# Output projection with earlier weight splits and delayed squares, and first GLA states copied on another engine

## The chip, the cores and the metric

The kernel runs on one core of one Trainium2 chip. The metric is the device time of one execution in microseconds (us); the median of several runs counts. Work is done by five engines, each with an instruction queue of its own that it works off in order: TensorE (PE in the profile; its weight loads are PEld), VectorE (DVE), ScalarE (ACT), GpSimd (POOL) and SyncE (SP, which here issues most DMAs). They wait for each other by semaphores.

## The reference

One decoder layer with two parallel branches, a retention and a gated linear attention (GLA), merged by sigmoid gates, then an output projection, the residual and a final RMS norm. D_MODEL is 1024, the sequence 512 with 16 meta tokens ahead of it, all in float32:

```python
u = rms_norm(h, norm_gain)
proj = u @ w_in            # rq, rk, rv, rg, gq, gk, gv, gg, glr, m_ret, m_gla
o_ret = retention_chunked(rope(rq), rope(rk) * scale, rv)
o_ret = head_group_norm(o_ret, ret_norm_gain) * silu(rg)
o_gla = gla_chunked(gq * scale, gk, gv, log_a)
o_gla = head_rms_norm(o_gla, gla_norm_gain) * silu(gg)
merged = sigmoid(m_ret) * (o_ret @ w_branch_ret) + sigmoid(m_gla) * (o_gla @ w_branch_gla)
h = h + merged @ w_out
out = rms_norm(h, final_norm_gain)[:, N_META:]
```

In the GLA scan each head carries a state (128 x 256) from block to block: `state = state * exp(a_n) + k_n^T v_n`. The kernel computes its first value from the meta tokens.

## The kernel before

**Float32 in three products.** Each operand is split in a high half (a cast to fp32r, on ScalarE) and a low half (operand minus high half, on VectorE): `split`, L164. A product is then three matmuls: high by high, high by low, low by high. For a weight tile of 128 x 1024 a split is one ScalarE CAST and one VectorE TENSOR_TENSOR.

**Seven products for eight.** `quad` (L267) computes a 2 x 2 block product with seven block products in place of eight. It loads the weight blocks w11, x3, w21, x1 and w22 (raw tiles; x3 and x1 get a second block added by an accumulating DMA from GpSimd), forms sums of them on VectorE (L388: w11 += x3; L395: w21 += w11) and runs the products in the order 1, 2, 6, 7, 5, 4, 3. They accumulate in three PSUM banks: 1, 6, 5 and 3 in `b` (the later ones on top of the earlier), 2 in `a`, 7 and 4 in `c`. After some of them bank contents are copied out on ScalarE (`copy`, L345 and L348) or handed to the caller's evacuation (`put`, which calls `evac`). `prepare(i, w)` takes a pair of weight buffers and issues the split of product i's weight, and notes it in `low`; without an earlier `prepare`, `product` issues it itself. There are three such pairs (`whi`, `wlo`, `bufs=3`), handed out in turn, so the split of one product has to wait until the product three before it is done. The flag `ahead` (set for retention heads 0 and 3, in their gate projection rg) issues the splits of products 2 and 4 sooner, `sooner` that of 6, `early` another order.

**Order of the work.** `weave(dense, chain)` runs a dense generator (a quad) and after each of its yields one step of a chain (other work), so the code's order is an interleaving of the two. `pend` holds functions with a count of steps after which `tick`, called at each yield of the dense part, runs them. The framework that places the instructions on the engines orders each queue by when it takes operations to be ready, and by the order of emission among those that are. `after(ins, prev)` fixes that one instruction stands behind another on its engine, without a wait; `pin` does this for PE between dense products.

**GLA attention** (`gla_attention(p)`, for two pairs of heads p = 0, 1) runs in blocks of 128 tokens. `meta_state3` (from L1005) multiplies for each head of the pair (`gs`, L1008), copies the result out of PSUM on VectorE to the state tile `gS` (L1010), and `values(0)` multiplies by it (`go`, L1019). For p = 1 this is woven into the gate projection gg of the second pair.

**Output projection** (from L1573). `wo_first` computes the first quarter of the columns (0 to 255) directly. Columns 256 to 767 are the quad `wo1`, with the chain `merged_sums` woven in, which makes the other operand's forms: S2 and S3, then S1, then S4, whose operand is made by the two L1556 operations, ordered behind the split noted in `low`. `evac_wo(n, th, p, q)` is the quad's evacuation: it adds the copied bank (L1637), adds into the residual tile `hs` (L1640 for n = 0, L1642 for n = 1), and calls `square` for two token tiles, which takes the sum of squares on ScalarE (L1592), scales and accumulates it on GpSimd (L1593) and for columns under 512 multiplies `hs` by the final gain on GpSimd (L1596). The quad calls it as put(0,0) after product 2, put(1,1) after 5, put(0,1) after 4 and put(1,0) after 3. The last quarter (columns 768 to 1023) uses `last`, two weight halves loaded and split by `wo_split` once the quad has been emitted; each token tile of it ends with the sum of squares, the norm and the output DMA.

Of the kernel before, what the change touches and what calls it, by code (L numbers as in the profile page):

```python
# [25 lines left out]
AF = mybir.ActivationFunctionType  # L26
# [84 lines left out]
def hybrid_kernel(ctx: ExitStack, tc: tile.TileContext, I, out: bass.AP):  # L111
    nc = tc.nc
# [55 lines left out]
    def after(ins, prev):  # L168

        tc.add_manual_dep(ins.ins, prev.ins.name, mybir.DependencyInfo(  # L170
            mybir.DependencyClass.NoSync, mybir.DependencyReason.DATA), reason="order on an engine")
# [42 lines left out]
    def weave(dense, chain, skip=0):  # L214

        for n, _ in enumerate(dense):
            tick()
            if n >= skip:
                next(chain, None)
        for _ in chain:  # L220
            pass
# [15 lines left out]
    def drain(*gens):  # L237
        for g in gens:
            for _ in g:
                tick()  # L240

    pend = []
    R = {}

    def tick():

        pend[:] = [(n - 1, f) for n, f in pend]
        while pend and pend[0][0] <= 0:
            pend.pop(0)[1]()
# [8 lines left out]
    def wraw(name, shape=(P, 4, 256)):  # L258
        return wp.tile(list(shape), F32, tag="raw", name=name, bufs=6)
# [5 lines left out]
    low = []  # L265

    def quad(cols, rows, name, evac, meta=None, adds=True, ahead=False, behind=None, src=None,  # L267
             forms=None, wide=False, sooner=False, early=False, home=None):

# [10 lines left out]
        src, forms = src or w_in, forms or (fh, fl)  # L282
# [4 lines left out]
        if adds:  # L287
            w11, w21, x3, x1, w22 = [wraw(f"{name}_{x}") for x in ("w11", "w21", "x3", "x1", "w22")]
            for t, kh, n in ((w11, 0, 0), (x3, 1, 1), (w21, 1, 0), (x1, 0, 0), (w22, 1, 1)):
                nc.sync.dma_start(t, block(kh, n))  # L290
                if t is x3 or t is x1:
                    x = nc.gpsimd.dma_start(t, block(0, 1), accum_op=ALU.add)  # L292
                    if t is x1 and behind is not None:
                        after(x, behind)
        else:
            w11, w21, w12, w22 = [wraw(f"{name}_{x}") for x in ("w11", "w21", "w12", "w22")]
# [15 lines left out]
        def prepare(i, w):  # L312
            hi, lo = wsplit([P, 4, 256], f"{name}_{i}")
            low[:] = split(hi, lo, w)
            return hi, lo
# [35 lines left out]
        def put(n, th, x, y):  # L351
            evac(n, th, x if wide else x[2], y)
# [10 lines left out]
        x = copy(b, 1)  # L363
        run_late()
        ready = prepare(2, w21) if ahead else None
# [5 lines left out]
        if early:  # L371
# [9 lines left out]
            ready = prepare(5, x1)  # L381
# [4 lines left out]
        else:  # L386
            product(2, A12, w21, a, True, ready)
            nc.vector.tensor_add(w11, w11, x3)  # L388
            ready = prepare(6, w11) if sooner else None
# [3 lines left out]
            ready = None  # L393
# [6 lines left out]
                late.append(lambda: meta(psm))  # L400
            yield
        product(5, S1, x1, b, False, ready)
        ready = prepare(4, w21) if ahead else None
        put(1, 1, b, x7)
        run_late()
        yield
        product(4, A22, w21, c, False, ready)
        ready = prepare(3, w22) if early else None
        put(0, 1, c, y)
        yield  # L410
        product(3, S4, w22, b, False, ready)
# [140 lines left out]
    ss = sp.tile([P, NTB + 1], F32, tag="ss5", name="ss5", bufs=1)  # L552
# [8 lines left out]
    for q in range(4):  # L561
        raw = wraw(f"gv0_{q}_w", (P, 2, 512))
        for s in (slice(0, 1), slice(1, 2)) if q < 2 else (slice(0, 2),):
            k0, n = 2 * q + s.start, s.stop - s.start
            x = (nc.sync if k0 else nc.scalar).dma_start(u[k0 // 4][:, k0 % 4:k0 % 4 + n], I["xt"][:, k0:k0 + n])
# [57 lines left out]
    for q in range(4):  # L623
        raw = graw[q]
        hi, lo = wsplit([P, 2, 512], f"gv0_{q}")
        for kk in range(2):
            kh, k = divmod(2 * q + kk, 4)
# [3 lines left out]
            if k == kh == 0:  # L631
                nc.vector.tensor_copy(hi[:, kk, :], raw[:, kk, :])
                w = nc.vector.tensor_sub(lo[:, kk, :], raw[:, kk, :], hi[:, kk, :].bitcast(F32))
            x = nc.vector.scalar_tensor_tensor(xl[kh][:, k, :, :HT], u[kh][:, k], g, xh[kh][:, k, :, :HT].bitcast(F32),
                                               op0=ALU.mult, op1=ALU.subtract)
# [5 lines left out]
        if q == 3:  # L641
            for kh in range(2):
                for k in range(4):
                    x = nc.scalar.activation(u[kh][:, k], u[kh][:, k], AF.Copy, scale=ng[:, 4 * kh + k:4 * kh + k + 1])
                    if kh == 1:
                        act(x)
                    else:
                        after(x, casts[-1])
                x = nc.vector.tensor_copy(um[:, 4 * kh:4 * kh + 4, :NM].rearrange("p k (h m) -> p k h m", h=2),
                                          u[kh][:, :, :, 256:HT])  # L650
# [6 lines left out]
        for t, kk, j in steps:  # L657
            kh, k = divmod(2 * q + kk, 4)
# [5 lines left out]
    def leave(t):  # L664
# [9 lines left out]
                                       accum_out=ss[:, NTB:]))  # L674
# [43 lines left out]
    forms = [form(S1, u11)]  # L718
# [207 lines left out]
    def gla_attention(p):  # L926
# [78 lines left out]
        def meta_state3():  # L1005
            for h in range(2):
                ps = pat(f"gs0{p}{h}")
                nc.tensor.matmul(ps[:, :256], S[h], vm[:, h * 256:(h + 1) * 256], start=True, stop=True)  # L1008
                s0 = gp.tile([P, 256], F32, tag="gS", name=f"gS{p}{h}", bufs=3)
                nc.vector.tensor_copy(s0, ps[:, :256])  # L1010
                S[h] = s0

        def values(b):
# [517 lines left out]
    def merged_sums():  # L1531

        a = [[sigr[2 * kh + j][:, :, th * 256:(th + 1) * 256] for j in range(2)] for th in range(2) for kh in range(2)]
        a00, a01, a10, a11 = a

        def parts_of(i, x, prev=()):
            for j in range(2):
                s = split(mforms[0][i][:, 2 * j:2 * j + 2], mforms[1][i][:, 2 * j:2 * j + 2], x[j])
                for ins, p in zip(s, prev):
                    after(ins, p)  # L1540

        for j in range(2):
            nc.vector.tensor_sub(a11[j], a11[j], a10[j])
            nc.vector.tensor_sub(a10[j], a00[j], a10[j])
        for j in range(2):
            nc.vector.scalar_tensor_tensor(a00[j], a11[j], -1.0, a00[j], op0=ALU.mult, op1=ALU.subtract)
        parts_of(S2, a00)
        yield
        parts_of(S3, a10)
        yield  # L1550
        yield
        parts_of(S1, a11, list(low))
        yield
        yield
        for j in range(2):
            after(nc.vector.scalar_tensor_tensor(a01[j], a00[j], -1.0, a01[j], op0=ALU.mult, op1=ALU.subtract), low[1])  # L1556
        parts_of(S4, a01, list(low))
        yield


# [11 lines left out]
    mforms = []  # L1572
# [7 lines left out]

    vs = {}

    def square(t, o):

        hh = hs[o // 512][:, t, o % 512:o % 512 + 256]
        sq = tmp(f"fsq{t}{o}")
        v = sp.tile([P, 1], F32, tag=f"fv{t}", name=f"fv{t}{o}", bufs=2)
        if o == 768:
            nc.vector.tensor_tensor_reduce(sq[:, :256], hh, hh, 1.0 / D, vs[t], ALU.mult, ALU.add, v)
        else:  # L1590
            ss = sp.tile([P, 1], F32, tag="ss", name=f"fss{t}{o}")
            nc.scalar.activation(sq[:, :256], hh, AF.Square, accum_out=ss)  # L1592
            nc.gpsimd.tensor_scalar(v, ss, 1.0 / D, vs.get(t, EPS), op0=ALU.mult, op1=ALU.add)  # L1593
        vs[t] = v
        if o < 512:
            nc.gpsimd.tensor_mul(hh, hh, fgb[:, o:o + 256])  # L1596
        if o < 768:
            return
        r = sp.tile([P, 1], F32, tag="rr", name=f"fr{t}")
        nc.gpsimd.tensor_tensor(r, v, mhalf, op=ALU.pow)  # L1600
        h0, h1 = hs[0][:, t, :], hs[1][:, t, :]
        nc.scalar.activation(h0, h0, AF.Copy, scale=r)
        w = 512 if t < NTB - 1 else 256
        for c in range(0, 512, w):
            nc.vector.scalar_tensor_tensor(h1[:, c:c + w], h1[:, c:c + w], r, fgb[:, 512 + c:512 + c + w],
                                           op0=ALU.mult, op1=ALU.mult)
            nc.sync.dma_start(out[t * P:(t + 1) * P, 512 + c:512 + c + w], h1[:, c:c + w])
        (nc.scalar if t == NTB - 1 else nc.sync).dma_start(out[t * P:(t + 1) * P, :512], h0)
# [6 lines left out]
    def wo_split(o, kh):  # L1615
        raw = wraw(f"wo{o}_w{kh}")
        nc.sync.dma_start(raw, I["w_out"][kh * 512:kh * 512 + 512, o:o + 256].rearrange("(k p) c -> p k c", p=P))
        w = wsplit([P, 4, 256], f"wo{o}_{kh}")
        split(*w, raw)
        return w  # L1620

    def wo_first():
        pss = [pat(f"wo0_p{t}") for t in range(NTB)]
        for kh in range(2):
            hi, lo = wo_split(0, kh)
            for t in range(NTB):
                for k in range(4):
                    mm3(pss[t][:, :256], *merged(4 * kh + k, t), hi[:, k], lo[:, k], kh == k == 0, kh == 1 and k == 3,
                        True)
                if kh:  # L1630
                    add(t, 0, pss[t])
            yield

    def evac_wo(n, th, p, q):
        d = hs[n][:, 2 * th:2 * th + 2, (256, 0)[n]:(512, 256)[n]]
        if q is not None:
            nc.vector.tensor_add(q, p, q)  # L1637
            p = q
        if n == 0:
            nc.vector.tensor_add(d, d, p)  # L1640
        else:
            nc.vector.scalar_tensor_tensor(d, p, -1.0, d, op0=ALU.mult, op1=ALU.add)  # L1642
        for t in (2 * th, 2 * th + 1):
            square(t, 256 + 256 * n)

    drain(wo_first())
    weave(quad((256, 512), True, "wo1", evac_wo, src=I["w_out"], forms=mforms), merged_sums())
    last = [wo_split(768, kh) for kh in range(2)]
    for t in range(NTB):
        ps = pat(f"wo2_p{t}")  # L1650
        for k in range(KD):
# [33 lines left out]
```

## Time and profile before

| | us |
|---|---|
| median of 3 runs | 744.87 |
| lowest, highest | 744.7, 747.28 |
| the profiled execution | 745.5 |
| its span (first to last instruction) | 743.7 |
| ScalarE busy | 448.8 |
| VectorE busy | 608.1 |

The granted TensorE clock is 0.999 of full speed. The views used below: the page (totals); the view of waits, whose columns are the waiting engine, tile and line, the one waited for, and us in total, times, longest; and the timeline, whose columns are the start in us from the beginning of the span, duration, engine, line, operation, output<-inputs, shapes and count, and in brackets the idle time ahead of it with what ended it. PE rows are the matmul's modelled duration, in which neighbours overlap; the distance from start to start is what one costs.

### The profile page before, as it was taken

The page shows a single profiled execution, that of the slowest core. Times are in us where ns is not written, and L with a number is a line of the kernel's source. Part 1 is how long each engine was busy: PE and PEld are TensorE (multiplying, and loading weights), DVE is VectorE, ACT ScalarE, POOL GpSimd, SP SyncE. Part 2 cuts the span into 40 slices and gives each one's busy share as a digit, 9 for nine tenths or more (in the row PEclk, how much of TensorE's full clock was granted, in tenths as well). Part 3 has the DMA queues.
Part 4 walks back from the last instruction along what each step waited for, and adds up shares of the span by engine and source line. Part 5 has one row for each costly group of instructions (what it writes and reads, how often), then busy time and mean ns, then how long its engine had stood idle before and what let it go on. Part 6 is the DMA issues. An engine that isn't in the chain of part 4 may idle for free.

```text
span 743.7 us, 14056 instructions
## 1 busy us (share of the span) xinstructions
PE 735.2 (99%) x5595; PEld 691.5 (93%) x5595; DVE 608.1 (82%) x881; ACT 448.8 (60%) x756; POOL 133.8 (18%) x174
## 2 busy tenths in 40 slices
PE   9999999999999999999999999999999999999996
PEld 6799999999999999999989999989999999988996
DVE  6699887689897789888957788967697999775995
ACT  7898674766875465546646555646555656532463
POOL 2112110112121120110520100540011201111132
PEclk9999999999999999999999999999999999999999
DMA  9873521832489973734783652795476357687503
GB/s 295 289 158 74 125 86 32 197 95 58 142 194 261 299 170 92 174 107 144 209 243 115 141 143 97 199 224 149 131 167 143 106 142 207 226 198 198 144 30 114
DMA packets 100250, 117.42 MB, mean 158 GB/s; under 512 B 5844, under 2 KB 90964, under 8 KB 99928
## 3 DMA queue, kind: packets, MB, share of 16 engines
q1 hardware_dynamic: 80008, 88.20, 37.5%
q0 software_dynamic: 19888, 27.79, 20.4%
q8 instruction: 44, 0.72, 0.4%
q10 hardware_dynamic: 288, 0.53, 0.2%
q14 instruction: 22, 0.18, 0.1%
HBM read 104.45 MB, written 11.53 MB: 156 GB/s over the span
## 4 chain that ended last, share of the span: by engine, by line
PE 89%; DVE 7%; issue 2%; ACT 1%; DMA 0%; POOLq 0%; POOL 0%; DVEq 0%
PE rqk_b L328 6%; PE rv_b L328 6%; PE rg_b L328 5%; PE rqk_c L328 5%; PE br_p L203 4%; PE br_p L202 4%; PE br_p L199 4%; PE mg_b L328 3%; PE mr_b L328 3%; PE gv_p L660 3%; PE rv_c L328 3%; PE bg_b L328 3%; PE rg_c L328 2%; PE gg_b L328 2%; PE gk_p L445 2%
## 5 line engine op out<-in xcount | busy, mean ns | idle before, releaser
L203 PE MATMUL br_p<-oh,br_l 128*128 128x512 f32 x128 | 49.9, 390 | 0.0
L202 PE MATMUL br_p<-ol,br_h 128*128 128x512 f32 x128 | 49.9, 390 | 0.0
L199 PE MATMUL br_p<-oh,br_h 128*128 128x512 f32 x128 | 49.8, 389 | 0.0
L164 ACT CAST rv_h<-rv_w 128x1024 fp32r<-128x1024 f32 x24 | 25.3, 1052 | 28.9 <-DVE rv_w L388 13.8
L328 PE MATMUL rqk_b<-xh,rqk_h 128*128 128x264 f32 (+1 forms) x128 | 36.2, 283 | 0.0
L328 PE MATMUL rqk_b<-xh,rqk_l 128*128 128x264 f32 (+1 forms) x128 | 36.1, 282 | 0.0
L328 PE MATMUL rqk_b<-xl,rqk_h 128*128 128x264 f32 (+1 forms) x128 | 36.0, 281 | 0.0
L164 DVE TENSOR_TENSOR rv_l<-rv_w,rv_h 128x1024 fp32r<-128x1024 f32 x24 | 29.3, 1223 | 8.1 <-ACT rv_h L164 8.1
L328 PE MATMUL rv_b<-rv_h,xh 128*128 128x256 f32 x128 | 35.8, 280 | 0.0
L328 PE MATMUL rg_b<-rg_h,xh 128*128 128x256 f32 x128 | 35.5, 278 | 0.2 <-DVE sg L852 0.2
L328 PE MATMUL rg_b<-rg_l,xh 128*128 128x256 f32 x128 | 35.7, 279 | 0.0
L328 PE MATMUL rv_b<-rv_l,xh 128*128 128x256 f32 x128 | 35.5, 278 | 0.0
L328 PE MATMUL rg_b<-rg_h,xl 128*128 128x256 f32 x128 | 35.4, 277 | 0.0
L328 PE MATMUL rv_b<-rv_h,xl 128*128 128x256 f32 x128 | 35.4, 277 | 0.0
L164 DVE TENSOR_TENSOR rg_l<-rg_w,rg_h 128x1024 fp32r<-128x1024 f32 x20 | 24.4, 1222 | 8.0 <-ACT rg_h L164 7.8
L292 POOL DMA_DIRECT2D rqk_x<-in_w_in_dram x8 | 10.4, 1302 | 111.7 <-DMA rqk_x<-in_w_in_dram 39.3
L164 ACT CAST rg_h<-rg_w 128x1024 fp32r<-128x1024 f32 x20 | 21.0, 1050 | 15.6 <-PE br_p L202 5.9
L203 PEld LDWEIGHTS br_p<-oh,br_l 128*128 128x128 f32 x128 | 24.0, 188 | 5.1
L164 ACT CAST rqk_h<-rqk_w 128x1024 fp32r<-128x1024 f32 x20 | 21.1, 1053 | 12.5 <-DVE rqk_w L388 4.7
L1411 ACT ACTIVATE on<-av,nm,g_r 128x512 f32<-128x512 f32 x16 | 12.5, 779 | 26.5 <-DVE nm L1409 26.5
L202 PEld LDWEIGHTS br_p<-ol,br_h 128*128 128x128 f32 x128 | 24.0, 188 | 4.6
L199 PEld LDWEIGHTS br_p<-oh,br_h 128*128 128x128 f32 x128 | 24.0, 188 | 4.5
(627 smaller groups left out, 3152.4 us busy)
## 6 DMA issues: line engine op xcount, KB each, us to landing
rv_w<-in_w_in_dram SPq DMA_DIRECT2D x16, 512.0 KB, 4.2
br_w<-in_w_branch_ret_dram SPq DMA_DIRECT2D x16, 512.0 KB, 3.4
rqk_w<-in_w_in_dram SPq DMA_DIRECT2D x12, 512.0 KB, 4.5
rg_w<-in_w_in_dram SPq DMA_DIRECT2D x12, 512.0 KB, 4.8
rqk_x<-in_w_in_dram SPq DMA_DIRECT2D x8, 512.0 KB, 5.5
rqk_x<-in_w_in_dram POOLq DMA_DIRECT2D x8, 512.0 KB, 8.2
rg_x<-in_w_in_dram SPq DMA_DIRECT2D x8, 512.0 KB, 4.1
rg_x<-in_w_in_dram POOLq DMA_DIRECT2D x8, 512.0 KB, 7.7
```

The source lines that it names most:

```text
L164: return nc.scalar.copy(hi, src), nc.vector.tensor_sub(lo, src, hi.bitcast(F32))
L199: m = nc.tensor.matmul(o, lh, rh, start=first, stop=False)
L202: nc.tensor.matmul(o, lh, rl, start=False, stop=False)
L203: m = nc.tensor.matmul(o, ll, rh, start=False, stop=last)
L292: x = nc.gpsimd.dma_start(t, block(0, 1), accum_op=ALU.add)
L328: m = nc.tensor.matmul(ps[t][:, :n] if wide else ps[t], l, r, start=first and j == 0, stop=kk == 3 and j == 2, skip_group_check=not fresh ...
L445: m = nc.tensor.matmul(pss[t][th], l[:, kk, c], r, start=first and j == 0, stop=kh == 1 and kk == 3 and j == 2, skip_group_check=not meta ...
L660: m = nc.tensor.matmul(pss[t], (al if j == 1 else ah)[t // 2, kh][:, k, c], (lo if j == 2 else hi)[:, kk, :], start=q == kk == j == 0, sto ...
L1411: nc.scalar.activation(on, ps, AF.Identity, scale=r, bias=nm)
```

## The change

- In `quad` a flag `tail`, set for `wo1` alone, issues the split of product 4's weight right after product 5 and ahead of put(1,1). The split of product 3's weight is issued right after product 4 and ahead of put(0,1), for `tail` and for `ahead` too (so in rg0 and rg3).
- In `merged_sums` the S4 step comes one yield sooner, and the two splits of the last quarter's weights (with their DMAs) are issued in the next step, after product 4 and before product 3.
- The squares of put(0,0) and put(1,1) are put off by 4 and 2 steps; those of all four puts are ordered on ScalarE behind the cast of the last prepared weight.
- In `meta_state3` the first states of the second pair (p = 1) are copied by ScalarE.

```diff
     def quad(cols, rows, name, evac, meta=None, adds=True, ahead=False, behind=None, src=None,
-             forms=None, wide=False, sooner=False, early=False, home=None):
+             forms=None, wide=False, sooner=False, early=False, home=None, tail=False):
...
         product(5, S1, x1, b, False, ready)
-        ready = prepare(4, w21) if ahead else None
+        ready = prepare(4, w21) if ahead or tail else None
         put(1, 1, b, x7)
         run_late()
         yield
         product(4, A22, w21, c, False, ready)
-        ready = prepare(3, w22) if early else None
+        ready = prepare(3, w22) if early or ahead or tail else None
         put(0, 1, c, y)
         yield
         product(3, S4, w22, b, False, ready)
...
                 s0 = gp.tile([P, 256], F32, tag="gS", name=f"gS{p}{h}", bufs=3)
-                nc.vector.tensor_copy(s0, ps[:, :256])
+                (nc.scalar.copy if p else nc.vector.tensor_copy)(s0, ps[:, :256])
                 S[h] = s0
...
         parts_of(S1, a11, list(low))
         yield
-        yield
         for j in range(2):
             after(nc.vector.scalar_tensor_tensor(a01[j], a00[j], -1.0, a01[j], op0=ALU.mult, op1=ALU.subtract), low[1])
         parts_of(S4, a01, list(low))
+        yield
+        last.extend(wo_split(768, kh) for kh in range(2))
         yield
...
-    def square(t, o):
+    def square(t, o, prev=None):
...
-            nc.scalar.activation(sq[:, :256], hh, AF.Square, accum_out=ss)
+            x = nc.scalar.activation(sq[:, :256], hh, AF.Square, accum_out=ss)
+            if prev is not None:
+                after(x, prev)
...
-        for t in (2 * th, 2 * th + 1):
-            square(t, 256 + 256 * n)
+        def squares():
+            for t in (2 * th, 2 * th + 1):
+                square(t, 256 + 256 * n, low[0])
+
+        if n == th:
+            pend.append(((4, 2)[n], squares))
+        else:
+            squares()
+
+    last = []
     drain(wo_first())
-    weave(quad((256, 512), True, "wo1", evac_wo, src=I["w_out"], forms=mforms), merged_sums())
-    last = [wo_split(768, kh) for kh in range(2)]
+    weave(quad((256, 512), True, "wo1", evac_wo, src=I["w_out"], forms=mforms, tail=True), merged_sums())
```

## The prediction

> **What bounds the kernel now.** I read the page first, then the chain of waits, then the timeline of single instructions at each place where TensorE waits.
>
> ```profile
> span 743.7 us, 14056 instructions
> PE 735.2 (99%) x5595; PEld 691.5 (93%) x5595; DVE 608.1 (82%) x881; ACT 448.8 (60%) x756; POOL 133.8 (18%) x174
> PE 89%; DVE 7%; issue 2%; ACT 1%; DMA 0%; POOLq 0%; POOL 0%; DVEq 0%
> ```
>
> TensorE (PE) is busy for 99% of the span, and it carries 89% of the chain that ended last. The change removes no matmul, so it can win only the time in which PE waits. The view of the waits on PE has four rows:
>
> ```profile
> PE warm_p L594 <- DVE warm L591: 1.2, 1, 1.2
> PE go L1019 <- DVE gS L1010: 0.6, 1, 0.6
> PE wo_p L202 <- DVE wo_l L164: 0.2, 1, 0.2
> PE rg_b L328 <- DVE sg L852: 0.2, 1, 0.2
> ```
>
> The first is the start of the program and stays. The second and third stand at lines which the change touches; the fourth is in a quad which it touches in passing. These numbers understate the loss: matmuls overlap, so a stall is read from start to start. Here is PE at the four places, each cut from its own window (start, duration, instruction):
>
> ```profile
> 163.25 0.28 PE L328 MATMUL gg_b<-gg_h,xl 128*128 128x256 f32 x1
> 164.09 0.70 PE L1019 MATMUL go<-gS,gQ 128*128 128x256 f32 x2 [0.56 <-DVE gS L1010]
> 164.62 0.59 PE L1020 MATMUL go<-gv,stb 128*128 128x256 f32 x2
> ...
> 592.86 0.28 PE L328 MATMUL rg_c<-rg_h,xl 128*128 128x256 f32 x1
> 593.32 0.36 PE L328 MATMUL rg_b<-rg_h,xh 128*128 128x256 f32 x1 [0.19 <-DVE sg L852]
> ...
> 722.77 0.28 PE L328 MATMUL wo_c<-wo_l,mh 128*128 128x256 f32 x1
> 722.88 0.28 PE L328 MATMUL wo_c<-wo_h,ml 128*128 128x256 f32 x1
> 723.27 0.36 PE L328 MATMUL wo_b<-wo_h,msh 128*128 128x256 f32 x1
> 723.46 0.28 PE L328 MATMUL wo_b<-wo_l,msh 128*128 128x256 f32 x1
> ...
> 727.45 0.28 PE L199 MATMUL wo_p<-wo_h,mh 128*128 128x256 f32 x1
> 727.98 0.39 PE L202 MATMUL wo_p<-wo_l,mh 128*128 128x256 f32 x1 [0.25 <-DVE wo_l L164]
> 728.20 0.28 PE L203 MATMUL wo_p<-wo_h,ml 128*128 128x256 f32 x1
> ```
>
> Undisturbed, one follows the other by 0.11 us (722.77 to 722.88). So:
> - first states: 163.25 to 164.09 is 0.84, less 0.11 is 0.73; the first pair takes 0.70 where the next takes 0.59, another 0.11, since the second copy is late too: **0.84**.
> - product 3 of the output projection: 722.88 to 723.27 loses 0.28, and the next step (0.19) 0.08: **0.36**. The view of waits doesn't list it.
> - last quarter: 727.45 to 727.98 loses 0.42, and the next step (0.22) 0.11: **0.53**.
> - product 3 of retention head 3's gate (rg): 592.86 to 593.32 loses **0.35**.
>
> Together 2.1 us, 0.28% of the span: that is nearly all there is to win.
>
> **First states on ScalarE.** ScalarE, then VectorE, then PE around them:
>
> ```profile
> 160.69 1.05 ACT L164 CAST gg_h<-gg_w 128x1024 fp32r<-128x1024 f32 x1
> 161.63 0.41 ACT L164 CAST lah<-la 128x256 fp32r<-128x256 f32 x1
> 163.56 1.05 ACT L164 CAST mr_h<-mr_w 128x1024 fp32r<-128x1024 f32 x1 [1.52 <-PE gg_b L328]
> ```
>
> ```profile
> 160.07 1.23 DVE L369 TENSOR_TENSOR mr_x<-mr_w,mr_w 128x1024 f32<-128x1024 f32 x1 [2.00 <-issue]
> 163.62 0.74 DVE L1010 COPY gS<-gs 128x256 f32<-128x256 f32 x2
> ```
>
> ```profile
> 160.84 0.70 PE L1008 MATMUL gs<-gvm,gkmt 128*128 128x256 f32 x2
> ```
>
> The second state lies in PSUM at 160.84+0.70 = 161.54. VectorE copies it at 163.62 only, because its queue first sat 2.00 us in front of mr_x and then worked off what had piled up. ScalarE is idle for 1.52 us until 163.56. The trace shows no copy of 128x256 from PSUM beside these; the nearest rows on ScalarE are the 128x256 cast (0.41) and, from above, the 128x512 copy out of PSUM below (0.57). I take 0.41 each. Behind the casts the copies run from about 162.04 to 162.9, with 0.57 each to 163.2. PE wants the first at 163.25+0.11 = 163.36, so both are in time: 0.84 gained. What is queued behind them on ScalarE is mr_h, which waits for PE until 163.56 anyway: no cost. That cover is gone if the copies stand behind mr_h (a rival below). VectorE loses 0.74 us of work; nothing is late next, since the go and gsu matmuls read, beside the states, only tiles of block 0, made earlier.
>
> By the Trainium skill ("ScalarE: Activation LUTs", What ACT_TABLE_LOAD costs) an ACTIVATE with immediate operands takes 186 ns + 0.833 ns per element, an estimate of 0.40 us for 256. The 0.41 of the cast agrees, and the sum would be the same.
>
> **The output projection.** The rows of ScalarE and then VectorE from product 6 on:
>
> ```profile
> 715.61 0.42 ACT L1592 ACTIVATE fsq<-hs 128x256 f32<-128x256 f32 x1 [2.19 <-DVE hs L1640]
> 716.42 0.57 ACT L348 COPY wo_x<-wo_b 128x512 f32<-128x512 f32 x1
> 716.89 1.05 ACT L164 CAST wo_h<-wo_w 128x1024 fp32r<-128x1024 f32 x1
> 718.31 1.07 ACT L164 CAST wo_h<-wo_w 128x1024 fp32r<-128x1024 f32 x1
> 720.22 1.23 ACT L164 CAST msh<-sigr 128x512 fp32r<-128x512 f32 x2 [0.83 <-DVE sigr L1556]
> 724.41 0.42 ACT L1592 ACTIVATE fsq<-hs 128x256 f32<-128x256 f32 x1 [2.01 <-issue]
> 725.22 1.04 ACT L164 CAST wo_h<-wo_w 128x1024 fp32r<-128x1024 f32 x1
> ```
>
> ```profile
> 717.98 1.60 DVE L164 TENSOR_TENSOR wo_l<-wo_w,wo_h 128x1024 fp32r<-128x1024 f32 x1 [1.27 <-ACT wo_h L164]
> 719.50 1.28 DVE L1556 SCALAR_TENSOR_TENSOR sigr<-sigr,sigr 128x512 f32<-128x512 f32 x2
> 720.71 1.21 DVE L164 TENSOR_TENSOR wo_l<-wo_w,wo_h 128x1024 fp32r<-128x1024 f32 x1
> ...
> 722.45 0.68 DVE L1637 TENSOR_TENSOR wo_x<-wo_b,wo_x 128x512 f32<-128x512 f32 x1
> ...
> 726.71 1.22 DVE L164 TENSOR_TENSOR wo_l<-wo_w,wo_h 128x1024 fp32r<-128x1024 f32 x1
> ```
>
> *Product 3's stall.* A product is 24 matmuls of 0.113, so 2.72 us. Product 4 ends at 722.88+0.28 = 723.16; counted back, 5 ends at 720.44, 7 at 717.72, 6 at 715.0. Product 3 adds into bank b and waits until VectorE has read product 5 out of it (L1637). That read is possible from 720.44 but runs at 722.45 to 723.13, 0.14 before the matmul. Ahead of it stand product 4's low half, the pair L1556, product 3's low half and a piece of the S4 form. That train starts late: 717.98 waited 1.27 us for its cast (716.89), which stood behind the copy of b (716.42), which stood behind two squares (from 715.61) that had waited for VectorE's sum.
>
> The change queues those squares behind product 4's cast. The copy then runs at 715.0 when 6 ends, and the cast from 715.5 to 716.6 (6 frees its weight buffer at 715.0). The low half runs at 716.6 to 717.8, L1556 until 719.0. Product 3's cast is held by 7's buffer (717.72) and stays near 718.31, its low half runs at 719.4 to 720.6. The two S4 pieces and L1637 are three operations of 0.68: in the worst order L1637 ends at 722.7, in the best at 721.3. To start at 722.99 PE needs it by 722.85. So the 0.36 goes in either order; in the worst the slack is 0.15. `prepare(3)` put ahead, and S4 one step sooner, give nothing by themselves: the trace has product 3's low half ahead of L1637 already, and S4 remains tied to product 4's split.
>
> *A hold by GpSimd.* The low half at 717.98 took 1.60, the same operation at 720.71 took 1.21. By the Trainium skill ("SBUF — State Buffer", Who interferes with whom) a VectorE instruction with two SBUF inputs contends with a GpSimd instruction that reads SBUF, and one of them blocks. The delayed squares send GpSimd's two gain multiplies into VectorE's train again, so by this rule 0.39 comes back and in the worst order leaves 0.24 of stall: the sum would be 1.5 instead of 1.7. That lies inside the range; the sum keeps the 0.36.
>
> *Last quarter's stall.* PE waits for the second weight's low half (726.71 to 727.93), whose cast (725.22) stood behind squares (724.41) that waited for a sum. Now the split is issued ahead of the last put, and these squares go after product 5's sum, about 722. The cast needs the buffer of product 4 (723.16), so runs to 724.2; with two sums of 0.68 ahead on VectorE the low half ends by 725.8. PE, 0.36 sooner, wants it at 727.2. The 0.53 goes, with 1.4 to spare. Both DMAs keep their order on SP; only outputs follow. At the end, the squares of the last put are behind a cast that is long done: no cost. GpSimd's scalar steps move with them.
>
> *Other quads.* The two gates with `ahead` (rg0, rg3) also split product 3's weight sooner. Bounds: the 0.35 stall of rg3 goes, or a low half of 1.21 gets in front of a read that product 3 waits for and costs 1.2. I take 0: cast and subtraction stay behind the same rope and turn work, which is emitted earlier in both programs.
>
> **Sum.** 0.84 + 0.36 + 0.53 = 1.73 us. The profiled execution took 745.5 (span 743.7 and 1.8 around it), 0.6 over the median of 744.87. It would be 743.8; from the median, **743.1 us**, 0.23% less.
>
> **Rivals.**
> - *rg3 too.* With product 3's split ahead, bank b there is read in time: a further 0.35 to 0.44, 742.7. For it: the stall has the same form. Against: the order argument above. Chance 0.12.
> - *Half of it does nothing.* The framework orders each engine by when it takes operations to be ready, so L1637 or the last cast can keep its place, or the copies run late: 744.0 (either 0.84 or 0.89 gained). Against: each has a slack worked out above, 0.15 at the least. Chance 0.17.
> - *ScalarE's queue in the projection, slower.* If the last quarter's second cast, issued sooner, is queued ahead of the two msh casts, ScalarE waits for product 4's buffer until 723.16, ends the cast at 724.2, msh's first half at 724.85, its low half on VectorE 0.68 later. Product 3 starts some 1.6 us later than now, its third matmul another 0.7: with the 0.84 of the first states and the 0.53 returned, 744.87 + 2.3 - 1.4 = 745.8. It decides as soon as that cast stands before msh at all. Against: msh is emitted a step earlier and ready near 719. Chance 0.07. The same for mr_h before the state copies: they end near 165.4, a stall of 1 us more instead of 0.84 less.
>
> **How the numbers follow.** Forecast 743.1 with 0.64, the rivals as above. The range: 742.0 (the rg3 case with half a us of scatter) to 745.8 (the slower rival). About 0.5% (3.7 us) is what a measurement of this kernel can tell from no change; no case reaches that on either side. For an order shifted elsewhere by the same edits I leave faster 0.05, slower 0.04, within 0.91.
>
> **What would show it.** Right: no row of PE waiting on gS; the two gS copies on ScalarE before mr_h; after the copy of b product 4's cast ahead of the squares; L1637 of product 5 ending before 722.2 (all shifted 0.84); the last low half ending over a us before PE wants it. Wrong: a new releaser in PE's waits, above all msh or wo_h; a row of rg_b waiting longer than 0.19.

## The result, and the profile after

| | before | after |
|---|---|---|
| median of 14 runs each, us | 744.84 | 744.0 |
| lowest, highest | 744.56, 747.28 | 743.02, 745.6 |
| the profiled execution (its span) | 745.5 (743.7) | 743.02 (741.2) |

The ratio is 0.9981, with a 95% interval of 0.9973 to 0.9989: about 1.4 us faster (0.8 to 2.0). The medians alone differ by 0.84. The profiled execution of the changed kernel was the fastest of its 14, and that of the kernel before stood 0.7 above its median, so the 2.5 us between their spans overstate the gain.

The page of the changed kernel, its totals:

```profile
span 741.2 us, 14057 instructions
PE 733.5 (99%) x5595; PEld 690.6 (93%) x5595; DVE 607.1 (82%) x879; ACT 449.5 (61%) x758; POOL 139.7 (19%) x174
```

Two VectorE instructions have become two of ScalarE, and PE does the same 5595 matmuls. The view of waits on PE, changed kernel, without the row of the start, which is as before:

```profile
PE rg_b L328 <- DVE sg L852: 0.2, 1, 0.2
PE gc L972 <- DVE gS L1025: 0.2, 1, 0.2
```

The rows of `go` and of `wo_p` are gone, that of rg stands as it was, and one is new: `gc` waits for a state update. PE at the four old places and the new one, timeline of the changed kernel:

```profile
162.69 0.28 PE L328 MATMUL gg_b<-gg_h,xl 128*128 128x256 f32 x1
162.80 0.59 PE L1019 MATMUL go<-gS,gQ 128*128 128x256 f32 x2
...
166.06 0.27 PE L976 MATMUL gc<-ident,gK 128*128 128x128 f32 x1
166.49 0.49 PE L972 MATMUL gc<-gQ,gK 128*128 128x128 f32 x2 [0.16 <-DVE gS L1025]
...
591.25 0.28 PE L328 MATMUL rg_c<-rg_h,xl 128*128 128x256 f32 x1
591.75 0.35 PE L328 MATMUL rg_b<-rg_h,xh 128*128 128x256 f32 x1 [0.22 <-DVE sg L852]
...
721.35 0.28 PE L328 MATMUL wo_c<-wo_h,ml 128*128 128x256 f32 x1
721.46 0.28 PE L328 MATMUL wo_b<-wo_h,msh 128*128 128x256 f32 x1
...
725.54 0.28 PE L199 MATMUL wo_p<-wo_h,mh 128*128 128x256 f32 x1
725.65 0.28 PE L202 MATMUL wo_p<-wo_l,mh 128*128 128x256 f32 x1
```

From start to start, `go`, `wo_b` and `wo_p` now follow at 0.11: the stalls of 0.84, 0.36 and 0.53 are gone. The second `gc` comes 0.43 behind its neighbour where 0.11 would be undisturbed, and its pair is 0.49 long where others are 0.39: 0.42 lost. The rg stall is 0.39.

Matched matmul by matmul, the two profiled executions shift against each other like this (minus: the changed kernel is ahead):

| where | shift, us |
|---|---|
| first loads, before 6 us | -0.53 |
| first `go` pair | -0.86 |
| second `gc` | +0.42 |
| rg0 and what lies up to the projection | -0.57 |
| product 3 of the projection | -0.36 |
| last quarter | -0.53 |

The first and fourth rows stand where every engine has the same instructions in the same order in both programs; they are taken up at the end. The other four add up to -1.33, beside the measured -1.4.

### The profile page after: what moved, and what is told of

It reads as the page before. It is cut to its first block, busy times and chain, and to the rows that moved or that the text cites. A ratio compares the mean times of both kernels' runs of the same rounds, so it can differ in the third digit from the quotient of the medians.

```text
span 741.2 us, 14057 instructions
## 1 busy us (share of the span) xinstructions
PE 733.5 (99%) x5595; PEld 690.6 (93%) x5595; DVE 607.1 (82%) x879; ACT 449.5 (61%) x758; POOL 139.7 (19%) x174
## 4 chain that ended last, share of the span: by engine, by line
PE 91%; DVE 5%; issue 2%; ACT 1%; POOL 0%; DMA 0%; POOLq 0%; DVEq 0%; ACTq 0%
PE rqk_b L328 6%; PE rv_b L328 6%; PE rg_b L328 5%; PE rqk_c L328 5%; PE br_p L202 4%; PE br_p L203 4%; PE br_p L199 4%; PE mg_b L328 3%; PE mr_b L328 3%; PE gv_p L660 3%; PE rv_c L328 3%; PE bg_b L328 3%; PE rg_c L328 2%; PE gg_b L328 2%; PE gk_p L445 2%
```

## The experiments

My theory after the result: the projection gained 0.89 through the squares alone, and half of the first states' 0.84 came back at `gc`, because VectorE's queue put other work ahead of the state update once the copies had left it. The rivals: that the gain of the projection comes from the sooner splits, and that `gc` is late for a reason which has nothing to do with VectorE's order. Lines of the experiments' kernels are shifted by up to eight.

One thing needs no run. The built program is that of the changed kernel, instruction for instruction, when `prepare(3)` loses its `ahead`, when the last quarter's splits are issued after the weave as before, and even when `prepare(4)` alone is left of the sooner steps in the projection: `prepare(3)` without its `tail`, S4 and the last quarter's splits where they were. These edits do nothing at all. `prepare(3)` can't lose its `tail` alone, though: with the last quarter's splits still issued sooner, the first of them then comes ahead of product 3's on ScalarE and VectorE. No run shows what that would cost.

**The first states alone** (before, with one line of the change):

```diff
-                nc.vector.tensor_copy(s0, ps[:, :256])
+                (nc.scalar.copy if p else nc.vector.tensor_copy)(s0, ps[:, :256])
```

> Only the two first-state copies move to ScalarE; the output projection is that of before. Theory (each stall has its own cause, and half of the gain of the copies is given back at the second block's score matmuls, because VectorE now takes the sum mr_w ahead of the state update that frees their bank): no stall at the first go matmul (0.84 before), a new one of 0.3 to 0.45 at the second gc L972, the output projection's 0.36 and 0.53 still there; time 0.4 us under before. Rival A (the new stall at gc is scatter of that one execution): no stall at gc, time 0.84 under before. Rival B (it comes from the other edits): no stall at gc either.

Measured: 745.45 beside 745.52, ratio 0.9999 (0.9991 to 1.0008). PE, then VectorE, timeline of this kernel:

```profile
167.14 0.27 PE L976 MATMUL gc<-ident,gK 128*128 128x128 f32 x1
167.98 0.49 PE L972 MATMUL gc<-gQ,gK 128*128 128x128 f32 x2 [0.57 <-DVE gS L1025]
```

```profile
160.70 1.23 DVE L369 TENSOR_TENSOR mr_x<-mr_w,mr_w 128x1024 f32<-128x1024 f32 x1 [2.11 <-DMA mr_w<-in_w_in_dram]
...
166.32 1.22 DVE L370 TENSOR_TENSOR mr_w<-mr_w,mr_w 128x1024 f32<-128x1024 f32 x1
167.45 0.48 DVE L1025 SCALAR_TENSOR_TENSOR gS<-gS,gto,gsu 128x256 f32<-128x256 f32 x1
```

No gain: the 0.84 at `go` is gone, but `gc` loses 0.84 less 0.11, and its pair (0.49 for 0.39) 0.10, which is 0.83. The state update (L1025), which frees the PSUM tile that `gc` writes next, stands behind `lal` and the sum into `mr_w`. So this part gives between nothing and half of its 0.84. How much hangs on when the DMA for the sum at the head of the train lands. Five profiled executions have the copies on ScalarE and VectorE's order of the changed kernel behind them (this one, the changed kernel's two, and the two with other squares or splits below). The sum started 0.15 and 0.12 us before the first `gs` matmul, or 0.16, 0.21 and 0.31 after it, and `gc` lost 0.37, 0.42, 0.70, 0.79 and 0.83.

**Everything but the first states** (changed kernel, that line as before):

> All of the change but the two copies, which stay on VectorE. Theory: the go stall of 0.84 is back, none at gc; both stalls of the output projection gone; time 0.89 us under before. Rival (the copies bring all of the gain, the output projection's stalls move elsewhere): time within 0.3 us of before.

Measured: 744.31, ratio 0.9986 (0.9976 to 0.9995), so 1.0 us. The view of waits on PE, this kernel, without the rows of the start and of rg, which are as before:

```profile
PE go L1019 <- DVE gS L1010: 0.8, 1, 0.8
```

The stall at `go` is back (1.13 from start to start, 0.29 more than before; the sum starts 0.28 later against the first `gs`), and that at `gc` is gone: the two belong together. Neither `wo_b` nor `wo_p` waits. The 1.0 agrees with the 0.89 of the two projection stalls.

**Squares as before** (changed kernel, sooner splits kept):

```diff
-                square(t, 256 + 256 * n, low[0])
+                square(t, 256 + 256 * n)
-        if n == th:
-            pend.append(((4, 2)[n], squares))
-        else:
-            squares()
+        squares()
```

> The changed kernel with the squares issued at once and without their order behind a cast; the splits and S4 stay sooner. Theory (the squares hold up the casts on ScalarE): product 4's cast stands behind the copy of b and the first squares again, and the last cast behind the second squares, so both stalls return, 0.2 to 0.36 ahead of product 3 and 0.3 to 0.53 in the last quarter. Rival (the splits issued sooner bring the gain): neither stall returns.

One execution, 745.29. ScalarE around product 6, timeline of this kernel, and its row of the last quarter in the view of waits on PE:

```profile
715.41 0.42 ACT L1593 ACTIVATE fsq<-hs 128x256 f32<-128x256 f32 x1 [2.19 <-DVE hs L1643]
...
716.23 0.57 ACT L348 COPY wo_x<-wo_b 128x512 f32<-128x512 f32 x1
```

```profile
PE wo_p L202 <- DVE wo_l L164: 0.3, 1, 0.3
```

The squares stand ahead of the copy of b again, and both stalls are back: 0.36 at product 3 (722.68 to 723.07, and the step behind it) and 0.53 at the last quarter (727.25 to 727.78, and the step behind it). The sooner splits without the squares give nothing.

**Squares put off, splits as before** (changed kernel):

```diff
-        ready = prepare(4, w21) if ahead or tail else None
+        ready = prepare(4, w21) if ahead else None
...
-        ready = prepare(3, w22) if early or ahead or tail else None
+        ready = prepare(3, w22) if early else None
...
         yield
+        yield
         for j in range(2):
...
-        last.extend(wo_split(768, kh) for kh in range(2))
-        yield
...
+    last.extend(wo_split(768, kh) for kh in range(2))
```

> The changed kernel with only the squares put off and the copies on ScalarE; splits of products 4 and 3, S4 and the last quarter's splits are issued where they were before. Theory (squares ahead of a cast make each stall): the last quarter's stall is gone, since the second squares stand behind the last cast; the first squares stand ahead of the copy of b and of product 4's cast again, so that product 3's stall of 0.36 is back. Rival (the splits issued sooner bring the gain): both stalls return, 0.36 and 0.53.

One execution, 744.45. ScalarE, then PE, timeline of this kernel:

```profile
714.67 0.42 ACT L1592 ACTIVATE fsq<-hs 128x256 f32<-128x256 f32 x1 [2.23 <-DVE hs L1642]
...
715.49 0.56 ACT L348 COPY wo_x<-wo_b 128x512 f32<-128x512 f32 x1
...
722.27 1.06 ACT L164 CAST wo_h<-wo_w 128x1024 fp32r<-128x1024 f32 x1 [0.80 <-ACT wo_h L164]
```

```profile
721.91 0.28 PE L328 MATMUL wo_c<-wo_h,ml 128*128 128x256 f32 x1
722.34 0.36 PE L328 MATMUL wo_b<-wo_h,msh 128*128 128x256 f32 x1 [0.15 <-DVE wo_x L1639]
```

The built program differs from the changed kernel's in one thing: the first two squares stand ahead of the copy of b and of product 4's cast. They are ordered behind the last *prepared* weight, and without `prepare(4)` that is an older one. So the last quarter's 0.53 is won by putting off the second squares alone, while product 3 loses 0.39 again (0.31 and 0.08): for product 3 the put-off squares and `prepare(4)` work only together. By the built programs above, these two are all of the projection's edits that count.

**The sum for mr0 behind the state update, in the kernel before.** The train on VectorE starts at the sum into `mr_x` (L369), for which the queue stands still until a DMA lands. If that is the cause of the stall at `go`, moving the sums of the next quad (mr0) away ends it with the copies still on VectorE:

```diff
+            s3 = nc.vector.tensor_add(x3, w22, w12)
+            s1 = nc.vector.tensor_add(x1, w12, w11)
+            if name == "mr0":
+                after(s3, G["state"])
+                after(s1, G["state"])
...
+                    if p == 1 and b == h == 0:
+                        G["state"] = s
```

> The kernel before with one thing moved: the two sums mr_x (L369) and mr_w (L370) are ordered on VectorE behind the first state update (L1025) of block 0. The copies of the first states stay on VectorE. Theory (VectorE's queue, held for about 2 us in front of mr_x by that operand's DMA, makes both the late copies and, in the changed kernel, the late state update): the copies end near 161.6 to 162, so the go stall of 0.84 is gone without the copies being moved, and no gc stall takes its place. Rival (VectorE is simply too full here and has to be relieved of the copies): a go stall of 0.3 or more stays.

One execution, 744.23. VectorE, then PE, timeline of this kernel:

```profile
161.91 0.75 DVE L1013 COPY gS<-gs 128x256 f32<-128x256 f32 x2
```

```profile
162.97 0.28 PE L328 MATMUL gg_b<-gg_h,xl 128*128 128x256 f32 x1
163.09 0.59 PE L1022 MATMUL go<-gS,gQ 128*128 128x256 f32 x2
```

The copies run 1.7 us earlier than in the kernel before, still on VectorE, where the whole program is 0.3 earlier, and `go` waits for nothing; nor does the second `gc`. The stall came from what stood at the head of the queue, not from the copies. But it was the sum itself more than the wait for its DMA: without the sum VectorE still stands idle for 1.71 us, until ScalarE's `gX` is there (159.49). So of the 2.00 us in front of `mr_x` only 0.3 were lost to the DMA, and another 1.14 to the sum (160.07 to 161.21). In place of the stall at `go`, mr0 loses 0.37 later (196.47 to 196.85, and the step behind it); matched matmul by matmul up to rg0, this version gains 0.53 of the 0.84.

**Changed kernel with sums moved.** Five versions were made to keep the gain at `go` without the loss at `gc`; the changed kernel itself was run again beside two of them. In all of them the sums and splits named stand behind the first state update of the second pair, as in the diff above.

*mr0's second sum (L370, into `mr_w`) and the low half of its first weight moved, and in rg0 and rg3 product 3's low half behind the read of bank b:*

```diff
+            if name == "mr0" and i == 1:
+                after(low[1], G["state"])
...
+            if name == "mr0":
+                after(s, G["state"])
...
+        if ahead:
+            after(low[1], R["total"])
```

> The changed kernel, with mr_w (L370) and the low half of mr0's first weight ordered on VectorE behind the first state update, and in rg0 and rg3 the low half of product 3's weight behind the read of bank b. Theory: the gc stall (0.32 to 0.74 in the runs so far) is gone, since 1.13 us less stands in front of the state update; the rg3 stall of 0.35 to 0.48 is gone or below 0.15; time 0.8 to 1.2 us under the changed kernel, ratio to before 0.997. Rival (the read of b in rg3 is late for another reason, or product 3 then waits for its low half): the rg3 stall stays at 0.35 or more.

*The same, and mr0's first sum (L369) too:*

> As the run before, and mr_x (L369) behind the first state update too, so that VectorE doesn't stand in front of its DMA. Theory: go, gc and rg3 free of stalls, as the run before; the idle time of VectorE in front of mr_x goes; time equal to the run before within 0.3 us, with a new stall in mr0 possible because its sums are made later. Rival (the DMA wait still costs PE time in the run before): 0.3 us or more under it.

*The changed kernel again:*

> The changed kernel once more beside the two runs above, for a comparison on one chip. Expected 0.9981 of before, 0.9973 to 0.9989; in the trace no go stall, a gc stall of 0.3 to 0.75, a rg3 stall of 0.35 to 0.5, none in the output projection.

Measured: 0.9987 (0.9975 to 0.9999), 0.9988 (0.9977 to 0.9998) and 0.9989 (0.9978 to 1.0000). No difference between the three. `gc` is free in the first two, but rg3 got worse. PE, timeline of the first of them:

```profile
592.40 0.28 PE L330 MATMUL rg_b<-rg_h,xh 128*128 128x256 f32 x1
593.30 0.38 PE L330 MATMUL rg_b<-rg_l,xh 128*128 128x256 f32 x1 [0.63 <-DVE rg_l L164]
```

The read of the bank is now in time, and product 3 starts undisturbed; its second matmul then waits for the low half that was put behind the read: 0.79 and 0.11 lost where 0.39 and 0.08 had been. Whichever of the two comes first on VectorE, the other is late. In the second of them mr0 loses another 0.37.

*Without the part in rg0 and rg3:*

> The changed kernel with only mr_w (L370) and the low half of mr0's first weight ordered on VectorE behind the first state update; rg0 and rg3 as in the changed kernel. Theory: go, gc and the output projection without stalls, rg3 at 0.35 to 0.48; 0.84 + 0.36 + 0.53 = 1.73 us under before, ratio 0.9977. Rival (the GLA part is made up for further on, where PE waits for weights instead): no more than the changed kernel, 0.9985 or above.

*As that one, with the rotation of q put behind one more yield in the retention heads 0 and 3, to make room for rg3's low half:*

```diff
+        if h % 3 == 0:
+            yield
         yield from rope(q, …)
-        if h % 3 == 0:
-            yield
```

> As the run before, and the rotation of q in heads 0 and 3 starts two steps later, so that three VectorE operations of 0.6 us leave the queue in front of the read of bank b in rg3 (one sum of the value weights, 1.13, moves up into their place). Theory: the read ends about 0.7 us sooner, so the rg3 stall of 0.35 to 0.48 is gone or below 0.1; 2.1 us under before, ratio 0.9972. Rival (the rotation then crowds VectorE in the value projection, and a low half there comes late): new stalls in rv_b or sc of 0.3 us or more, ratio as the run before or above.

Measured: 743.6 beside 745.69, ratio 0.9973 (0.9964 to 0.9982), and 749.65, ratio 1.0046 (1.0032 to 1.0060). The first is the best version so far. Of its profile: `go` loses nothing, the `gc` behind it 0.25, and a later `gc` (188.59 to 189.25) loses 0.55 where the kernel before loses 0.15, so by its profiled execution it would win 1.1, not the 2.0 (1.3 to 2.7) of the ratio. The second came out the other way. The view of waits on PE, then VectorE, kernel with the later rotation:

```profile
PE rg_b L330 <- DVE sg L856: 4.1, 2, 2.2
```

```profile
281.94 1.23 DVE L371 TENSOR_TENSOR rv_x<-rv_w,rv_w 128x1024 f32<-128x1024 f32 x1 [3.46 <-DMA rv_w<-in_w_in_dram]
...
284.21 0.68 DVE L856 TENSOR_TENSOR sg<-rg_b,rg_x 128x512 f32<-128x512 f32 x1
```

The room that the rotation left was taken by the next quad's sum `rv_x`, and VectorE stood 3.46 us in front of its DMA with the low half and the read of bank b queued behind. It is `mr_x` again, and here the wait itself counts: PE lost 2.34 in rg0 and 2.10 in rg3. The stall in `rv_b` that the rival named came as well, 0.67 at 609.3.

*Only mr0's first sum (L369) moved; and the best version so far once more:*

```diff
+            s = nc.vector.tensor_add(x3, w22, w12)
+            if name == "mr0":
+                after(s, G["state"])
```

> The changed kernel with mr_x (L369) alone ordered on VectorE behind the first state update, so that VectorE no longer stands in front of that operand's DMA. Theory: no idle of about 2 us in VectorE's queue ahead of block 1's products, state update done before the second gc wants its bank, so go and gc free of stalls; 0.84 + 0.89 = 1.73 us under before (ratio 0.9977), less up to 0.4 where mr0's sums are now made later. Rival (the low half mr_l, which now stands ahead of the update, holds it up as mr_w did): a gc stall of 0.3 or more stays.

> The kernel of run e9 once more, on the same chip as the run above. By its trace (go gone, 0.15 at the second gc in place of 0.3 to 0.75, a new 0.4 at a later gc) it gains 0.3 us or less on the changed kernel: ratio 0.9978 to 0.9983. If its 0.9973 was more than scatter: 0.9975 or under.

Measured, beside 745.84: 743.62, ratio 0.9975 (0.9966 to 0.9983), and 743.75, ratio 0.9974 (0.9964 to 0.9985). VectorE, then PE, timeline of the version with only L369 moved:

```profile
160.40 0.69 DVE L963 TENSOR_TENSOR gK<-gX,gk 128x512 f32<-128x512 f32 x1 [1.71 <-ACT gX L957]
...
166.42 0.47 DVE L1027 SCALAR_TENSOR_TENSOR gS<-gS,gto,gsu 128x256 f32<-128x256 f32 x1
```

```profile
167.25 0.27 PE L978 MATMUL gc<-ident,gK 128*128 128x128 f32 x1
167.36 0.39 PE L974 MATMUL gc<-gQ,gK 128*128 128x128 f32 x2
```

With the sum behind the state update (it runs at 166.81), VectorE's idle time ends with work that is ready (`gK`), and `gc` follows at 0.11. In the other one, the later `gc` loses 0.23 this time, 0.08 more than in the kernel before: the size of that stall, like that of the first, changes from one execution to the next. By the stalls at the places of the change the version with only L369 moved wins the full 1.73 (0.84, 0.36 and 0.53), beside 1.9 measured (1.3 to 2.5); the changed kernel by its two traces 1.3 and 1.4. The span of that profiled execution, 743.3, doesn't show the gain: it started 0.6 later, and low halves behind a DMA wait of VectorE came late in rqk (0.39 lost at 249.75) and in rg0 (0.59 at 272.93). Whether the moved sum has a part in the two was not tried. The three ratios (0.9973, 0.9974 and 0.9975) all lie below the two of the changed kernel (0.9981 and 0.9989), but the intervals overlap: that these versions beat the changed kernel is likely, not shown. These three beat the kernel before.

## Why the prediction was right, point by point

**The total.** Forecast 743.1 from a median of 744.87, a gain of 1.73; measured 744.0, with a gain of 1.4 by the ratio. 0.42 of the 1.73 came back at the second `gc` in the profiled execution, and 0.37 to 0.83 in the five with this order; the rest of the gap between 743.1 and 744.0 lies within the scatter of the medians (744.84 to 745.84 for the kernel before in the five sets of runs). The range of 742.0 to 745.8 holds no change at all too, so that the time fell inside it says little; the stalls, place by place, say more. And the 0.5% that the prediction held a measurement to need was too cautious: the intervals here are 0.1% to either side.

**Product 3, 0.36: right, and by the mechanism named.** ScalarE, then VectorE, timeline of the changed kernel:

```profile
713.50 0.59 ACT L348 COPY wo_x<-wo_b 128x512 f32<-128x512 f32 x1 [1.62 <-PE wo_b L328]
713.98 1.05 ACT L164 CAST wo_h<-wo_w 128x1024 fp32r<-128x1024 f32 x1
714.94 0.41 ACT L1593 ACTIVATE fsq<-hs 128x256 f32<-128x256 f32 x1
...
721.70 1.06 ACT L164 CAST wo_h<-wo_w 128x1024 fp32r<-128x1024 f32 x1 [1.66 <-PE wo_c L328]
725.30 0.42 ACT L1593 ACTIVATE fsq<-hs 128x256 f32<-128x256 f32 x1 [2.55 <-DVE hs L1643]
```

```profile
715.12 1.21 DVE L164 TENSOR_TENSOR wo_l<-wo_w,wo_h 128x1024 fp32r<-128x1024 f32 x1
...
717.79 1.43 DVE L164 TENSOR_TENSOR wo_l<-wo_w,wo_h 128x1024 fp32r<-128x1024 f32 x1 [0.25 <-ACT wo_h L164]
...
719.74 0.68 DVE L1640 TENSOR_TENSOR wo_x<-wo_b,wo_x 128x512 f32<-128x512 f32 x1
...
723.40 1.21 DVE L164 TENSOR_TENSOR wo_l<-wo_w,wo_h 128x1024 fp32r<-128x1024 f32 x1
...
728.65 0.48 DVE L1590 CUSTOM_DVE_ANT_0 fsq<-hs,fv 128x256 f32<-128x256 f32 x1 [1.14 <-POOL fv L1596]
```

The copy of b and product 4's cast come ahead of the squares, and the low half starts at 715.12. The whole program is 1.53 us earlier here (product 4 ends at 721.63, not 723.16), and 1.53 taken off the predicted 715.0, 715.5 and 716.6 gives 713.5, 714.0 and 715.1, the rows above. The read of product 5 (L1637 of before is L1640 here) ends at 720.42. On the prediction's scale that is 721.95, between its best order (721.3) and its worst (722.7), with 0.9 to spare before the matmul wants it at 721.32. One emphasis was missing: it held that `prepare(3)` and the sooner S4 "give nothing by themselves", which the built programs bear out, but it priced `prepare(4)` only through the squares. The run with the splits as before shows that the squares move only if `prepare(4)` comes sooner.

**A hold by GpSimd.** Product 3's low half (717.79 to 719.22) took 1.43 beside GpSimd's multiply (716.95 to 718.14) and scalar step (718.13 to 719.88), where the rows above with the same shape took 1.21. By the rule of the Trainium skill ("SBUF — State Buffer", Who interferes with whom) the hold was to come back, and the trace agrees, with 0.22 in place of the 0.39 seen before. It took 0.22 of a slack of 0.9 and cost PE nothing.

**Last quarter, 0.53: right.** The last low half ends at 724.61 and PE wants it at 725.65: 1.04 to spare, where 1.4 was forecast. The reason was half the one given: the cast is free because the second squares stand elsewhere, not because the split is issued ahead of the last put. And the squares did not go "after product 5's sum, about 722": all six that were left run from 725.30 on, behind the sum of put(0,1). That made something late which the prediction didn't name: the first token tile of the last quarter waits 1.14 us for GpSimd (the L1590 row). The last tile makes it up; from the last matmul to the end both programs take 6.0 us.

**First states, 0.84: right at its place, wrong in what follows.** ScalarE, then VectorE, timeline of the changed kernel:

```profile
160.14 0.38 ACT L1010 COPY gS<-gs 128x256 f32<-128x256 f32 x1
...
161.36 0.38 ACT L1010 COPY gS<-gs 128x256 f32<-128x256 f32 x1
...
163.00 1.05 ACT L164 CAST mr_h<-mr_w 128x1024 fp32r<-128x1024 f32 x1 [0.95 <-PE gg_b L328]
```

```profile
164.49 0.41 DVE L164 TENSOR_TENSOR lal<-la,lah 128x256 fp32r<-128x256 f32 x1
164.82 1.22 DVE L370 TENSOR_TENSOR mr_w<-mr_w,mr_w 128x1024 f32<-128x1024 f32 x1
165.96 0.47 DVE L1025 SCALAR_TENSOR_TENSOR gS<-gS,gto,gsu 128x256 f32<-128x256 f32 x1
```

The copies took 0.38 (forecast 0.41), both ahead of `mr_h`, and `go` starts 0.84 sooner. The step that failed is "VectorE loses 0.74 us of work; nothing is late next". It looked at what `go` and `gsu` read, and not at the tile that `gsu` fills and `gc` takes next, which the state update has to free. In the kernel before, that update ran right behind `gsg`; here `lal` and the sum into `mr_w` have been ordered between them, 1.47 us of work (164.49 to 165.96), more than the copies had taken. Its reading of the late copies was half right too: most of the 2.00 us in front of `mr_x` were idle in any case, and the sum itself cost more than the wait, as the run with the sums moved shows. The sign that the prediction named for itself, "no row of PE waiting on gS", did catch the new stall: the row of `gc` is one.

**rg0 and rg3, taken as 0: right**, and for a stronger reason than the one given: the orders are identical. The rg3 stall, 0.35 before, is 0.37 to 0.40 in the runs that left it alone.

**The rivals.** The one with rg3 gained did not come, nor did the slower one in ScalarE's queue: both `msh` casts run at 717.66, the last quarter's second cast at 721.70. "Half of it does nothing" (744.0, by a late copy or a kept order) gave the measured median, but not its mechanism: all three stalls went, and one came.

## What to carry to other kernels

Work that leaves an engine's queue leaves a place, and the framework fills it with what it takes to be ready: look up which instruction moves up, and who waits for the one that it passes. Before moving work off a "late" engine, look at the head of its queue: here a sum that nobody needed yet held VectorE, for the wait on its DMA and for its own 1.14 us, and putting that one sum behind the urgent update removed the same stall, in the changed kernel without a new one at these places. An edit that leaves the built program as it was can be priced at nothing before any run.

## What the runs showed of the hardware

**The clock falls after a wait of some 2 us, but not always.** In the run with the later rotation PE stood still twice. The view of windows of that kernel (stretch and its length in us; busy time and count of PE, PEld, DVE, ACT and POOL; then the granted clock, the DMA share and GB/s):

```profile
282.00:285.00 3.00, 0.86 (x8) 0.67 (x6) 3.00 (x4) 0.07 (x1) 0.00 (x0) 1.00 0.00 0
285.00:290.00 5.00, 4.96 (x32) 4.71 (x36) 5.00 (x8) 3.00 (x6) 0.00 (x0) 0.66 0.38 105
...
596.00:600.00 4.00, 2.07 (x18) 1.90 (x18) 4.00 (x6) 1.85 (x3) 0.00 (x0) 1.00 0.33 86
600.00:605.00 5.00, 5.00 (x60) 3.94 (x59) 5.00 (x8) 1.63 (x4) 0.57 (x1) 1.00 0.23 66
```

After the first stall (2.34 us) the clock was 0.66 over the next 5 us, which is what 3.4 us at half speed make, and from 285.97 to 289.17 the 15 steps from one matmul to the next took 0.21 each in place of 0.11: some 1.5 us more on top of the stall. After the second (2.10 us) it stayed at 1.00. By the Trainium skill ("TensorE: Matmul & The Clock Gate", Part 1: The HAM clock gate) the clock is halved after an idle window of about 3.4 us, and the windows run freely. The 3.4 us at half speed agree with one such window; the idle time of 2.34 us is shorter than the window that the Trainium skill names. Whether the place of the stall in the window decided between the two was not tried.

**Start-up and one DMA scatter by half a us.** The -0.53 of the first 6 us and the -0.57, which falls in rg0, stand where all orders agree. In rg0 it hangs on a load: VectorE's sum of `rg_w` waited 1.60 us for the DMA of `rg_x` in the profiled execution of before, and 0.35 in that of the changed kernel; low halves that come late in the first are in time in the second. Across the profiled executions with the same order there, the start lay between 0.53 sooner and 0.72 later than in before. A gain of under half a us can't be read from two spans; it takes the stalls, place by place, or many runs.
